# Gate and query products of a hybrid decoder step by seven block products for each pair, with gates and retention's output kept in DRAM

## The chip, the cores and the metric

The kernel runs on one core of one Trainium2 chip. The metric is the device time of one execution in microseconds (us), as the median of several runs. All arithmetic is on 32-bit floats. Matrix products are made on TensorE from operands that are split into a rounded part and a remainder (fp32r), so that one product of full precision takes three matmuls: rounded x rounded, rounded x remainder, remainder x rounded.

## The reference, cut to what matters

Two layers work on 512 prompt tokens and 64 sample tokens (8 sequences of 8), 1024 channels:

```
rq, rk, rv, rg, sq, sk, sv, mq, g_ret, g_swa, g_mem = split(x @ w_in)
ret_b = (silu(rg) * group_norm(retention(rq, rk, rv))) @ w_br_ret
swa_b = window_attention(sq, sk, sv) @ w_br_swa
mem_b = memory_attention(mq, mem_k, mem_v) @ w_br_mem
merged = sigmoid(g_ret) * ret_b + sigmoid(g_swa) * swa_b + sigmoid(g_mem) * mem_b
x = layer_norm(ALPHA * x + merged @ w_out)
h = square(relu(x @ w_up))
x = layer_norm(ALPHA * x + h @ w_down)
```

The three gates are 1024 channels wide each, mq is 512 wide.

## The kernel before, in words

Activations lie channel by token, in two groups of 288 tokens, A and B (32 sample and 256 prompt tokens each). Weights come as units of 128 x 8 x 128 numbers, 154 for a layer, in the order of `unit_order`: a unit multiplies 1024 input channels into 128 output channels, or (`bs`, `bm`, `dh`) 512 into 256. `fetch` loads a raw unit on SP's queue; `split` turns it into the rounded half (ScalarE or VectorE) and the remainder, either by one VectorE subtraction or, for units split more than FAR us ahead, by a negated copy on ScalarE and an accumulating DMA of the raw weights issued by GpSimd. `mstep` multiplies a unit with one token group (24 matmuls of 288 columns, or 12 for half the input channels) into a PSUM bank of tag `g`, of which there are three, and hands it to an evacuation function; `both` does so for A and B.

The instructions of each engine stand in the order in which the program is written. `run` writes a list of steps. After each six matmuls `Filler.advance` is called, which inserts pieces of other work: generators for retention, window attention (`swa_prompt`, `swa_sample`), memory attention (`mem_prompt`, `mem_sample`) and norms, each cut at its yields and continued when a built-in estimate of the engines' times says that its operands are nearly ready. Generators of one lane go one after the other. `finish` and `drain` write what is left of them at once. `tick` splits weights ahead, up to `2 * cap` halves alive.

All larger tiles share one pool of 38 buffers (tag `T`). PSUM banks of tag `a` (five) serve attention and retention.

In `layer` the order is: memory keys and values (mk, mv), retention's inputs with retention beside them, sv, sk, sq; then a `drain`; then eight times a unit of gr and a unit of br (window attention beside it); four units of mq; four times two units of gs and one of bs (memory attention beside it); four times two of gm and one of bm; wo with the first norm; up; down. A gate is Tanh of its product, kept in one of four small tiles `t` until the branch's product is evacuated: `br_ev` writes (t + 1) * product into `mg`, `add_ev` adds to it and, for bm, writes the rounded half and the remainder that wo reads.

The up product of the later six eighths is made by `pair_steps`: two units are multiplied with both groups by seven block products of 12 matmuls, in place of eight (Winograd's form of Strassen's scheme, blocks: two output units by two halves of the input channels; token groups A and B). `block` makes the seven weight operands of a pair from its two raw units, three of them sums; `sums` makes the four sums of activation blocks. In `pair_steps` the seven products are combined by subtractions on VectorE. There, each pair is followed by two units of dh.

Of the kernel before, what the change touches and what calls it, by code (L numbers as in the profile page):

```python
# [32 lines left out]
ORDER_DH = (0, 2, 1, 3)  # L33
SKEW_WO = 8
# [5 lines left out]
FAR = 11.0  # L40
DN_SKEW = 7
# [25 lines left out]
def unit_order():  # L67
# [21 lines left out]
def pack_weights(w_in, w_br_ret, w_br_swa, w_br_mem, w_out, w_mem_kv, w_up, w_down):  # L89
# [13 lines left out]
    for l in range(DEPTH):  # L103
        wb_swa = w_br_swa[l][swa_rows]
        for u, key in enumerate(order):
# [29 lines left out]
            elif k == "up":  # L135
                v = full(w_up[l], m * P + np.arange(P))
            elif k in ("ua", "ub"):
# [88 lines left out]
def items():  # L226


    r = []
    for l in range(DEPTH):  # L230
        for i, k in enumerate(unit_order()):
            u = l * UNITS + i
            if k[0] == "ua":
                r += [(u + 1, (l,) + k, b) for b in range(BLOCKS)]
            elif k[0] != "ub":
                r.append((u, (l,) + k, None))
    return r


def plan(todo):  # L240
# [3 lines left out]
    while i < len(todo):  # L244
# [12 lines left out]
        else:  # L257
            out.append(t)
            t += {"mk": c, "mv": c, "ua": n / 2}.get(k, 2 * n)
# [190 lines left out]
class Builder:  # L450
# [24 lines left out]
    def dram(self, shape):  # L475
        self.n += 1
        return self.dr.tile(shape, F32, tag=f"d{self.n}", name=f"d{self.n}", bufs=1)
# [73 lines left out]
    def split(self, i):  # L551
# [8 lines left out]
        if self.use[i] - self.fill.t > FAR and k[1] not in ("mq", "gs", "bs", "gm", "bm") and u > 15 \  # L560
# [9 lines left out]
    def block(self, u, b):  # L570


        V = self.nc.vector
        ra, rb = self.raw[u - 1], self.raw[u]
# [14 lines left out]
        if b == 5 and self.items[self.split_next][1][2] == 7:  # L589
# [70 lines left out]

    def pair_steps(self, key, XT, evac):

# [42 lines left out]
        def e6():  # L705
# [3 lines left out]
                step(2, lambda: (bank("x", "a"), True, e2)), step(3, lambda: (bank("y", "a"), True, e3)),  # L709
# [3 lines left out]
    def sums(self, y, T):  # L713
# [4 lines left out]
        for h in range(2):  # L718
            q = slice(2 * h, 2 * h + 2)
            b11, b21, b12, b22 = y["A"][0][:, q], y["A"][1][:, q], y["B"][0][:, q], y["B"][1][:, q]  # L720
# [7 lines left out]
            for i in range(2):  # L728
# [3 lines left out]
                V.tensor_tensor(t[i][1], r[i], t[i][0].bitcast(F32), ALU.subtract)  # L732

# [283 lines left out]
    def retention(self, l, p, qk, rv, rvs, sg, GR):  # L1017
# [159 lines left out]
        for g_ in "AB":  # L1177
# [4 lines left out]
            self.nc.vector.tensor_tensor(lo, src, hi.bitcast(F32), ALU.subtract)  # L1182

# [35 lines left out]
    def swa_prompt(self, l, c, sq, sk, sv, SW):  # L1219
# [62 lines left out]
        for kb in range(kb0, 2):  # L1282
            for kv in range(2):
# [3 lines left out]
        yield from self.hi_lo(SW[g]["h"][0][:, :, a:a + P], SW[g]["l"][0][:, :, a:a + P],  # L1287
                              ps.rearrange("p (i q) -> p i q", i=4))

    def swa_sample(self, l, sq, sk, svs, SW):  # L1290
# [43 lines left out]
        for f in range(2):  # L1334
# [13 lines left out]
            cs = slice(SOFF[g], SOFF[g] + 32)  # L1348
            hi = SW[g]["h"][0][:, :, cs].rearrange("p g (b t) -> p g b t", b=4)
            lo = SW[g]["l"][0][:, :, cs].rearrange("p g (b t) -> p g b t", b=4)  # L1350
            yield from self.hi_lo(hi, lo, o)
# [129 lines left out]
    def layer(self, l, X):  # L1481
# [3 lines left out]
        uid = {k: self.item[(l,) + k, None] for k in unit_order() if k[0] not in ("ua", "ub")}  # L1485
# [64 lines left out]

        GR = {g: {"h": [], "l": []} for g in "AB"}
# [123 lines left out]
        steps += self.both(uid["sv", 0], X, sv_ev) + self.both(uid["sk", 0], X, sk_ev)  # L1675
        for m in range(4):
# [6 lines left out]
        mg = [self.pair_tiles(), self.pair_tiles()]  # L1683
        SW = self.feat_tiles(1)
        for c in range(4):
            self.fill.add(self.swa_prompt(l, c, sq, sk, sv, SW), 3)
        self.fill.add(self.swa_sample(l, sq, sk, svs, SW), 3)
        ts = {}

        def gate_ev(m):  # L1690
            def ev(g, ps):
                t = self.tt()[:, :NG[g]]
# [278 lines left out]
```

## Time and profile before

| | |
|---|---|
| median of 3 runs | 2159.79 us (2156.87 to 2160.55) |
| the profiled execution | 2157.69 us |
| its span, first to last instruction | 2155.9 us |
| granted TensorE clock, mean share | 0.992 |
| TensorE busy | 2118.5 us, 98% |
| VectorE, ScalarE, GpSimd busy | 59%, 43%, 11% |
| DMA | 292.42 MB, mean 136 GB/s |

The span leaves out what lies around the first and the last instruction. Busy times of pipelined instructions overlap by some hundredths of a us each.

### The profile page before, as it was taken

The numbers are of one execution on the slowest core, as the hardware profiler recorded it, in microseconds if no ns is written. First come the engines' busy times: TensorE is split into PE (matmuls) and PEld (weight loads), VectorE is DVE, ScalarE is ACT, GpSimd is POOL, SyncE is SP. The second block draws the span as 40 slices with busy tenths as digits, with TensorE's granted clock in tenths as the row PEclk, the third lists the DMA queues.
The fourth block names the chain that finished last, engine by engine and source line by source line (L and its number), as shares of the span: only waits on it lengthen the run. The fifth ranks groups of instructions, "written<-read, shape, count | busy, mean of one in ns | idle before, by whom it ended". The sixth has DMA issues, their size and how long they took to land.

```text
span 2155.9 us, 39206 instructions
## 1 busy us (share of the span) xinstructions
PE 2118.5 (98%) x16180; PEld 2058.2 (95%) x16180; DVE 1261.5 (59%) x2705; ACT 925.6 (43%) x1750; POOL 232.9 (11%) x297
## 2 busy tenths in 40 slices
PE   9999999999999999999989999999999999999997
PEld 8999999999999999999989999999999999999997
DVE  6455644456547576765745556444565565767766
ACT  4333355322256444446553333562221665444452
POOL 0111111000022000000321111000000220000012
PEclk9999999999999999999999999999999999999999
DMA  8455645434375422225895556544342854222242
GB/s 316 114 143 134 166 118 120 145 109 144 119 211 127 126 94 84 79 88 151 204 266 143 144 141 174 122 114 132 135 157 85 229 120 130 79 79 99 98 122 60
DMA packets 87618, 292.42 MB, mean 136 GB/s; under 512 B 9552, under 2 KB 19280, under 8 KB 87376
## 3 DMA queue, kind: packets, MB, share of 16 engines
q0 software_dynamic: 31408, 113.79, 24.0%
q1 hardware_dynamic: 50944, 168.27, 22.8%
q10 hardware_dynamic: 5088, 7.87, 1.1%
q8 instruction: 127, 2.08, 0.4%
q14 instruction: 51, 0.42, 0.1%
HBM read 200.89 MB, written 15.99 MB: 101 GB/s over the span
## 4 chain that ended last, share of the span: by engine, by line
PE 91%; DVE 4%; issue 2%; DMA 2%; ACT 1%; POOL 0%; SPq 0%; DVEq 0%; POOLq 0%; ACTq 0%
PE pg L359 69%; PE pa L359 23%; DVE T L359 3%; DMA T<-T 1%; ACT T L359 1%; DVE u L359 0%; DMA T<-in_wall 0%; ACT u L359 0%; DMA T<-in_memT 0%; SPq L359 0%; DVE ln L359 0%; DVE accA L359 0%; DVE s L359 0%; POOL T L359 0%; POOL rc L359 0%
## 5 line engine op out<-in xcount | busy, mean ns | idle before, releaser
L359 PE MATMUL pg<-T,T 128*128 128x288 f32 (+1 forms) x11840 | 1643.3, 297 | 19.3 <-ACT T L359 10.9
L359 PEld LDWEIGHTS pg<-T,T 128*128 128x128 f32 x11840 | 1591.4, 190 | 44.4 <-ACT T L359 17.0
L359 PE MATMUL pa<-T,T 128*128 128x288 f32 (+8 forms) x3368 | 449.5, 303 | 2.4 <-DVE u L359 2.4
L359 ACT CAST T<-T 128x1024 fp32r<-128x1024 f32 (+6 forms) x464 | 354.6, 789 | 210.1 <-DVE T L359 174.7
L359 PEld LDWEIGHTS pa<-T,T 128*128 128x128 f32 (+3 forms) x3368 | 399.7, 176 | 23.0 <-issue 9.5
L359 DVE TENSOR_TENSOR T<-T,T 128x512 fp32r<-128x512 f32 (+8 forms) x418 | 361.9, 878 | 85.2 <-ACT T L359 75.4
L359 POOL DMA_DIRECT2D T<-T x145 | 124.7, 868 | 1379.2 <-ACT T L359 1013.2
L359 ACT ACTIVATE T<-T 128x1024 fp32r<-128x1024 f32 (+2 forms) x157 | 165.3, 1054 | 10.5 <-DVE T L359 8.2
L359 ACT ACTIVATE t<-pg 128x288 f32<-128x288 f32 x128 | 52.6, 411 | 215.8 <-PE pg L359 210.5
L359 ACT ACTIVATE u<-u 128x288 f32<-128x288 f32 x200 | 89.0, 445 | 96.0 <-DVE u L359 92.0
L359 DVE TENSOR_TENSOR T<-u,T 128x288 fp32r<-128x288 f32 x160 | 72.4, 454 | 78.0 <-ACT T L359 78.0
L359 ACT COPY T<-pg 128x512 f32<-128x512 f32 (+2 forms) x44 | 20.8, 479 | 213.0 <-PE pg L359 213.0
L359 DVE TENSOR_TENSOR T<-T,pg 128x288 f32<-128x288 f32 x128 | 57.7, 451 | 75.6 <-PE pg L359 75.1
L359 ACT CAST T<-u 128x288 fp32r<-128x288 f32 x160 | 69.3, 433 | 52.6 <-DVE u L359 48.6
L359 DVE TENSOR_TENSOR T<-T,u 128x288 f32<-128x288 f32 (+2 forms) x136 | 88.1, 660 | 3.8
L359 DVE SCALAR_TENSOR_TENSOR T<-t,pg 128x288 f32<-128x288 f32 x64 | 29.0, 453 | 94.0 <-ACT t L359 76.2
L359 DVE TENSOR_TENSOR T<-T,pa 128x288 f32<-128x288 f32 (+1 forms) x92 | 52.1, 567 | 25.1 <-PE pa L359 23.7
L359 DVE TENSOR_TENSOR T<-pa,T 128x512 fp32r<-128x512 f32 (+2 forms) x48 | 24.9, 533 | 64.9 <-ACT T L359 64.7
L359 DVE SCALAR_TENSOR_TENSOR u<-t,pg 128x288 f32<-128x288 f32 x64 | 28.8, 450 | 55.8 <-PE pg L359 55.2
L359 DVE TENSOR_TENSOR u<-u,pa 128x288 f32<-128x288 f32 x72 | 32.6, 453 | 35.2 <-PE pa L359 35.0
L359 ACT CAST T<-pa 128x512 fp32r<-128x512 f32 (+2 forms) x44 | 19.4, 451 | 70.2 <-PE pa L359 66.3
L359 DVE CAST T<-T 128x1024 fp32r<-128x1024 f32 (+1 forms) x71 | 45.2, 641 | 1.0 <-DMA T<-in_wall 1.0
(164 smaller groups left out, 1095.3 us busy)
## 6 DMA issues: line engine op xcount, KB each, us to landing
T<-in_wall SPq DMA_DIRECT2D x305, 512.0 KB, 4.2
T<-T POOLq DMA_DIRECT2D x141, 512.0 KB, 5.7
T<-in_mck POOLq DMA_DIRECT2D x16, 512.0 KB, 4.4
T<-in_mcv POOLq DMA_DIRECT2D x16, 512.0 KB, 6.6
T<-in_s POOLq DMA_DIRECT2D x8, 512.0 KB, 8.2
out_state_s<-T POOLq DMA_DIRECT2D x8, 512.0 KB, 3.8
T<-in_xT SPq DMA_DIRECT2D x4, 576.0 KB, 10.4
T<-in_xT ACTq DMA_DIRECT2D x4, 576.0 KB, 6.8
```

Source lines behind the costliest of these rows:

```text
L359: r = f(*a, **kw)
```

## The change

The 24 gate units and the four of mq become 14 pairs (`xa`, `xb` in the weights' order), multiplied by `pair_steps` in one stage behind sq: four pairs of gs, four of gr, four of gm, two of mq. Weight blocks 0, 4 and 5 of a pair get their remainder from ScalarE and an accumulating DMA where they are split more than 8 us ahead. The sums of x's blocks are made by `sums` from x in DRAM, loaded anew on GpSimd's queue, from the third unit of sq on. The Tanh of a pair's products goes into one tile and from there to DRAM by ScalarE's queue; it is loaded again on SP's queue a step before its use. Retention's output `GR` is stored to DRAM by GpSimd's queue and loaded before the last bs unit has run; window attention's output goes through DRAM too. Behind the pairs come bs (four units), br (eight) and bm (four) without gates between them, memory attention beside bs and br. mk and mv are reloaded by GpSimd's queue in place of ScalarE's. The diff, cut:

```diff
+PAIRS = [((k, 2 * i), (k, 2 * i + 1)) for k, n in (("gs", 4), ("gr", 4), ("gm", 4), ("mq", 2)) for i in range(n)]
+FAR_BLOCK = 8.0
@@ unit_order
-    for m in range(8):
-        o += [("gr", m), ("br", m)]
-    o += [("mq", m) for m in range(4)]
-    for g, b in (("gs", "bs"), ("gm", "bm")):
-        for i in range(4):
-            o += [(g, 2 * i), (g, 2 * i + 1), (b, i)]
+    for j in range(len(PAIRS)):
+        o += [("xa", j), ("xb", j)]
+    o += [("bs", i) for i in range(4)] + [("br", m) for m in range(8)] + [("bm", i) for i in range(4)]
@@ split
-        if self.use[i] - self.fill.t > FAR and k[1] not in ("mq", "gs", "bs", "gm", "bm") and u > 15 \
+        if self.use[i] - self.fill.t > FAR and k[1] not in ("bs", "br") and u > 15 \
                 and (k[1] != "dh" or k[2] == 0):
@@ block
+        key, far = self.items[self.split_next][1], self.use[self.split_next] - self.fill.t
...
-        if b == 5 and self.items[self.split_next][1][2] == 7:
+        if b == 5 and key[1:3] == ("ua", 7) or b in (0, 4, 5) and key[1] == "xa" and far > FAR_BLOCK:
             self.nc.scalar.activation(w[:, 4:8], src, AF.Copy, scale=-1.0)
             self.nc.gpsimd.dma_start(w[:, 4:8], src, accum_op=ALU.add)
@@ pair_steps
-    def pair_steps(self, key, XT, evac):
+    def pair_steps(self, key, XT, evac, xbank="a"):
...
-                step(2, lambda: (bank("x", "a"), True, e2)), step(3, lambda: (bank("y", "a"), True, e3)),
+                step(2, lambda: (bank("x", xbank), True, e2)), step(3, lambda: (bank("y", "a"), True, e3)),
@@ sums
-    def sums(self, y, T):
+    def sums(self, parts, T):
...
+            b11, b21, b12, b22 = parts(h)
+            yield (b11, b21, b12, b22)
@@ retention, at the end
+            if p % 2:
+                for k in "hl":
+                    nc.gpsimd.dma_start(self.grd[g_, k, p // 2], GR[g_][k][p // 2])
@@ swa_prompt, at the end (swa_sample alike)
-        yield from self.hi_lo(SW[g]["h"][0][:, :, a:a + P], SW[g]["l"][0][:, :, a:a + P],
-                              ps.rearrange("p (i q) -> p i q", i=4))
+        st = self.tile([P, 2, 4, P], F32R)
+        yield from self.hi_lo(st[:, 0], st[:, 1], ps.rearrange("p (i q) -> p i q", i=4))
+        nc.gpsimd.dma_start(SW[:, :, :, OFF[g] + a:OFF[g] + a + P], st)
@@ layer
+        def reload(h):
+            t = [self.tile([P, 4, 288]) for _ in range(2)]
+            for i, g in enumerate("AB"):
+                for j in range(2):
+                    nc.gpsimd.dma_start(t[i][:, 2 * j:2 * j + 2],
+                                        src[:, 4 * j + 2 * h:4 * j + 2 * h + 2, OFF[g]:OFF[g] + NG[g]])
+            return [t[i][:, 2 * j:2 * j + 2] for i in range(2) for j in range(2)]
+        tx = self.sums(reload, Ts)
         for m in range(4):
...
+            if m == 2:
+                steps.append(([], lambda: self.fill.add(tx, 1), 0.0))
             steps += self.both(uid["sq", m], X, sq_ev)
+        del GR
         self.run(steps)
         self.fill.drain()
...
+        def gate_pair(j):
+            st = []
+            def ev(i, g, ps):
+                if not st:
+                    st.append(self.tile([P, 4, 288]))
+                S.activation(st[0][:, 2 * i + "AB".index(g)], ps, AF.Tanh, scale=0.5)
+                if (i, g) == (0, "B"):
+                    nc.scalar.dma_start(gd[j], st.pop())
             return ev
...
+        for j in range(12):
+            steps += self.pair_steps((l, "xa", j), XT, gate_pair(j), "g")
+        steps.append(([], load_sw, 0.0))
+        for j in range(2):
+            steps += self.pair_steps((l, "xa", 12 + j), XT, mq_pair(j), "g")
+            if j == 0:
+                steps.append(([], lambda: self.fill.add(mem_parts(), 2), 0.0))
+        self.run(steps, 3.5)
         self.fill.drain()
+        del X, XT, Ts, sq, sk, sv, svs, skv
...
+        def gate(j):
+            def fn():
+                t = self.tile([P, 4, 288])
+                nc.sync.dma_start(t, gd[j])
...
+        def load_gr():
+            for h in range(2):
+                for g in "AB":
+                    for k in "hl":
+                        t = self.tile([P, 4, 288], F32R)
+                        nc.gpsimd.dma_start(t, self.grd[g, k, h])
+                        GR[g][k].append(t)
+        steps = [gate(0)]
         for i in range(4):
-            for m in (2 * i, 2 * i + 1):
-                steps += self.both(uid["gs", m], X, gate_ev(m))
+            steps.append(gate(i + 1))
             for e in range(2):
-                steps += self.both(uid["bs", i], SW, add_ev(2 * i + e), range(4 * e, 4 * e + 4))
+                steps += self.both(uid["bs", i], SW, first_ev(2 * i + e), range(4 * e, 4 * e + 4))
+            if i == 2:
+                steps.append(([], load_gr, 0.0))
         self.run(steps, 2.5)
...
+        for m in range(8):
+            if m % 2 == 0:
+                steps.append(gate(5 + m // 2))
+            steps += self.both(uid["br", m], GR, add_ev(1, m))
+        steps.append(([], lambda: [self.fill.finish(gen) for gen in mem], 0.0))
+        self.run(steps, 2.5)
...
         for i in range(4):
+            if i < 3:
+                steps.append(gate(9 + i))
             if i == 3:
                 steps.append(([], load_y, 0.0))
-            for m in (2 * i, 2 * i + 1):
-                steps += self.both(uid["gm", m], X, gate_ev(m))
-            if i == 0:
-                steps.append(([], lambda: [self.fill.finish(gen) for gen in mem], 0.0))
             for e in range(2):
-                steps += self.both(uid["bm", i], ME, add_ev(2 * i + e, M2), range(4 * e, 4 * e + 4))
+                steps += self.both(uid["bm", i], ME, add_ev(2, 2 * i + e, M2), range(4 * e, 4 * e + 4))
```

`first_ev` writes (t + 1) * product into `mg`, as `br_ev` did; `load_sw` drains the fillers and loads window attention's output by four GpSimd transfers.

## Rows read from the trace of the kernel before

**Rows 1.** The page: busy time of the engines, granted clock in 40 slices.

```profile
PE 2118.5 (98%) x16180; PEld 2058.2 (95%) x16180; DVE 1261.5 (59%) x2705; ACT 925.6 (43%) x1750; POOL 232.9 (11%) x297
...
PEclk9999999999999999999999999999999999999999
```

**Rows 2.** Timeline, ScalarE among gm units: start, length (us), engine, operation, idle before.

```profile
566.51 0.41 ACT L359 ACTIVATE t<-pg 128x288 f32<-128x288 f32 x1 [2.79 <-PE pg L359]
569.71 0.41 ACT L359 ACTIVATE t<-pg 128x288 f32<-128x288 f32 x1 [2.79 <-PE pg L359]
```

**Rows 3.** Windows: gr/br; gs/bs with memory attention; start and rest of pairs.

```profile
core 0: us, PE busy (x) PEld busy (x) DVE busy (x) ACT busy (x) POOL busy (x), PEclk, DMA share, GB/s
...
727.00:750.00 23.00, 23.00 (x175) 23.00 (x174) 20.70 (x34) 8.19 (x11) 1.11 (x3) 1.00 0.43 112
750.00:996.00 246.00, 246.00 (x1847) 246.00 (x1847) 173.00 (x308) 105.70 (x214) 0.90 (x1) 1.00 0.28 92
283.30:407.50 124.20, 124.20 (x976) 118.27 (x974) 56.15 (x132) 68.08 (x151) 12.12 (x15) 1.00 0.52 128
437.00:551.00 114.00, 113.52 (x979) 109.50 (x978) 67.84 (x151) 31.04 (x83) 8.82 (x16) 1.00 0.43 148
```

**Rows 4.** Instruction groups by shape: count, busy us, mean ns, idle before.

```profile
L359 DVE TENSOR_TENSOR T<-T,T 128x512 fp32r<-128x512 f32 x144 | 98.0, 687 | 32.3 <-ACT T L359 31.8
L359 ACT CAST T<-T 128x512 fp32r<-128x512 f32 x148 | 87.3, 618 | 128.8 <-DVE T L359 120.0 <-PE pg L359 4.4 <-DMA T<-in_memT 4.4
L359 ACT ACTIVATE t<-pg 128x288 f32<-128x288 f32 x128 | 52.6, 411 | 215.8 <-PE pg L359 210.5 <-issue 4.9
L359 DVE TENSOR_TENSOR T<-T,T 128x1024 f32<-128x1024 f32 x24 | 29.2, 1218 | 0.0
L359 DVE TENSOR_TENSOR u<-pg,u 128x288 f32<-128x288 f32 x24 | 11.0, 457 | 3.2 <-PE pg L359 3.2
```

**Rows 5.** Timeline, first layer: first and last instructions of the sums behind up.

```profile
727.64 2.88 DVE L359 TENSOR_TENSOR T<-T,T 128x576 f32<-128x576 f32 x4
...
740.68 1.95 DVE L359 TENSOR_TENSOR T<-T,T 128x1152 fp32r<-128x1152 f32 x2
```

**Rows 6.** DMA: software queue's packets, MB, share; issues with KB, landing; GpSimd's issue time.

```profile
q0 software_dynamic: 31408, 113.79, 24.0%
...
T<-in_wall SPq DMA_DIRECT2D x305, 512.0 KB, 4.2
T<-T POOLq DMA_DIRECT2D x141, 512.0 KB, 5.7
...
L359 POOL DMA_DIRECT2D T<-T x145 | 124.7, 868 | 1379.2 <-ACT T L359 1013.2 <-PE pg L359 268.0 <-PE pa L359 54.7
```

**Rows 7.** Timeline, end of sq: retention's last remainders, the last rope.

```profile
273.54 1.42 DVE L359 TENSOR_TENSOR T<-T,T 128x576 fp32r<-128x576 f32 x2
...
281.54 0.48 DVE L359 STREAM_SHUFFLE u<-pg 128x288 f32<-128x288 f32 x1
```

**Rows 8.** Timeline, memory attention: first step, start of second sample part, last step.

```profile
437.16 0.71 ACT L359 CAST T<-T 128x256 fp32r<-128x256 f32 x2
...
538.33 0.89 DVE L359 TENSOR_TENSOR T<-T,cst 128x128 f32<-128x128 f32 x4
...
550.75 0.29 DVE L359 TENSOR_TENSOR T<-pa,T 128x128 fp32r<-128x128 f32 x1 [0.72 <-ACT T L359]
```

**Rows 9.** Timeline, bm: two evacuations in a row; ScalarE's reloads of x.

```profile
571.32 0.45 DVE L359 SCALAR_TENSOR_TENSOR u<-t,pg 128x288 f32<-128x288 f32 x1 [5.71 <-PE pg L359]
573.14 0.45 DVE L359 SCALAR_TENSOR_TENSOR u<-t,pg 128x288 f32<-128x288 f32 x1
...
596.95 2.62 ACTq L359 DMA_DIRECT2D T<-in_xT  x4
```

**Rows 10.** Windows of 10 us with TensorE idle: columns as in Rows 3.

```profile
1010.00:1020.00 10.00, 7.06 (x49) 6.39 (x48) 4.77 (x10) 7.13 (x14) 0.84 (x1) 1.00 0.96 297
1080.00:1090.00 10.00, 7.11 (x38) 6.15 (x37) 2.81 (x5) 6.41 (x10) 3.79 (x5) 0.83 1.02 276
```

More of the change, by code (lines that the diff above doesn't have):

```diff
@@ L136, in pack_weights @@
                 v = full(w_up[l], m * P + np.arange(P))
+            elif k in ("xa", "xb"):
+                f, g = (full(w_in[l], COLS[c] + i * P + np.arange(P)) for c, i in PAIRS[m])
+                if k == "xb":
+                    f, g = g, f
+                v = np.concatenate([f[:, :4], g[:, 4:]], 1)
             elif k in ("ua", "ub"):
@@ L732, in sums, with operands, part, tsum @@
                 V.tensor_tensor(t[i][1], r[i], t[i][0].bitcast(F32), ALU.subtract)
+    @staticmethod
+    def operands(X, T):
+        def part(g, j):
+            return lambda i: (X[g]["h"][j][:, i, :], X[g]["l"][j][:, i, :])
+        def tsum(a, b):
+            return lambda i: tuple(T[i // 2][a][e][:, 2 * b + i % 2, :] for e in range(2))
+        return [part("A", 0), tsum(1, 0), tsum(0, 1), tsum(0, 0), part("A", 1), tsum(1, 1), part("B", 1)]
     def pair_tiles(self, dt=F32):
@@ L1347, in swa_sample @@
             g = "AB"[f]
[L1348 to L1351, printed above, removed]
+            st = self.u(256).bitcast(F32R).rearrange("p (k g t) -> p k g t", k=2, g=4)
+            yield from self.hi_lo(*(st[:, k].rearrange("p g (b t) -> p g b t", b=4) for k in range(2)), o)
+            nc.gpsimd.dma_start(SW[:, :, :, f * 544:f * 544 + 32], st)
     def mem_prompt(self, h, mq, mk, mv, ME, ahead=None):
@@ L1484, in layer @@
         ident = self.c("ident")
-        uid = {k: self.item[(l,) + k, None] for k in unit_order() if k[0] not in ("ua", "ub")}
+        uid = {k: self.item[(l,) + k, None] for k in unit_order() if k[0] not in ("ua", "ub", "xa", "xb")}
         M = self.M
@@ L1549, in layer @@
         self.run(steps, 2 * CAP_M if l else CAP_M)
+        self.grd = {(g, k, h): self.dram([P, 4, 288], F32R) for g in "AB" for k in "hl" for h in range(2)}
+        swd = self.dram([P, 2, 4, TOK], F32R)
+        gd = [self.dram([P, 4, 288]) for _ in range(12)]
+        src = self.I["xT"] if l == 0 else self.xs
         GR = {g: {"h": [], "l": []} for g in "AB"}
@@ L1715, in mem_parts, with load_sw @@
                 yield (parts[0],)
[L1716 to L1724 removed]
+                V.tensor_tensor(parts[1], t, parts[0].bitcast(F32), ALU.subtract)
+        SW = {g: {} for g in "AB"}
+        def load_sw():
+            self.fill.drain()
+            for g in "AB":
+                for i, k in enumerate("hl"):
+                    SW[g][k] = [self.tile([P, 4, 288], F32R)]
+                    nc.gpsimd.dma_start(SW[g][k][0], swd[:, i, :, OFF[g]:OFF[g] + NG[g]])
+        steps = []
+        for j in range(12):
[6 more added lines that the diff above has]
+        self.run(steps, 3.5)
         self.fill.drain()
+        del X, XT, Ts, sq, sk, sv, svs, skv
         ME = self.feat_tiles(1)
@@ L1823, in layer @@
         Ts = []
-        tg = self.sums(y, Ts)
+        tg = self.sums(lambda h: [y[g][j][:, 2 * h:2 * h + 2] for g in "AB" for j in range(2)], Ts)
         def dh(q, k, src):
@@ L1848, in layer @@
         del tg
-        def part(g, j):
-            return lambda i: (X1[g]["h"][j][:, i, :], X1[g]["l"][j][:, i, :])
-        def tsum(a, b):
-            return lambda i: tuple(Ts[i // 2][a][e][:, 2 * b + i % 2, :] for e in range(2))
-        XT = [part("A", 0), tsum(1, 0), tsum(0, 1), tsum(0, 0), part("A", 1), tsum(1, 1), part("B", 1)]
-        for k in "hl":
-            X1["B"][k][0] = None
+        XT = self.operands(X1, Ts)
         H.pop(0)
```

77 lines of the change are left out of this document (35 added, 42 removed).

## The prediction

> **What bounds the kernel now.** First the totals on the page [rows 1]: TensorE is busy for 2118.5 of 2155.9 us, at a granted clock that stands at nine tenths or more in every slice; the other engines have room. So a matmul fewer is worth its own time, if nothing new makes TensorE wait. Next the pace: in the gm stage one gate product (24 matmuls of 288 columns) ends every 3.20 us [rows 2], 0.133 us a matmul; I use 1.60 us for 12 matmuls and 6.40 us for a unit (48). Third, the stretches of the first layer that are rearranged [rows 3]: TensorE is busy for 124.20 of 124.20 us where gates and br alternate and for 113.52 of 114.00 where memory attention runs. Nothing waits there now, so there is nothing to gain but matmuls, and every wait that the new order makes is a loss.
>
> **What is removed.** 24 gate units and 4 of mq become 14 pairs in each layer. A pair of units took 2 x 48 = 96 matmuls and takes 7 x 12 = 84 afterwards, all of 288 columns. That is 12 x 14 x 2 = 336 matmuls fewer, 28 x 1.60 = 44.8 us: 22.4 a layer. From the profiled execution's 2157.69 us this alone gives 2112.9.
>
> **What is added, per layer.**
>
> *VectorE and ScalarE in the pair stage.* A pair needs seven remainders of 512 elements (0.687 each), one sum of 1024 (1.218), two of 512 and five subtractions of 288 (0.457) [rows 4]: 4.81 + 1.22 + 1.37 + 2.29 = 9.7 us of VectorE. Window attention runs beside it; in the first stretch of [rows 3] VectorE was busy for 56.15 us, of which 16 evacuations of about 0.45 are br's, so at most 49 us are attention, 4.1 a pair over 12 pairs. TensorE has 11.2 us a pair, and attention's matmuls (124.2 - 16 x 6.4 = 21.8 us) add 1.8: 13.0. VectorE asks for 13.8, or 11.7 where the three remainders of blocks 0, 4 and 5 go to ScalarE and GpSimd (3 x 0.687 less). The nearest row is the start of the existing pair stage, where VectorE was busy for 20.70 of 23.00 us, 90%, and TensorE all 23.00 [rows 3]. 11.7 of 13.0 is the same 90%. ScalarE has seven casts (0.618), a copy, four Tanh (0.411), the three extra passes and attention, some 8 + 2.5 us, and fits. So from 0 to 12 x 0.8 = 9 us; I take **1**, since the row at 90% lost nothing.
>
> *Start of the pair stage.* Block 1 needs the sums of x from both halves, 1.6 us after the stage begins; block 0 alone covers them. The same sums stand in the trace behind up: from 727.64 to 742.63, some 15 us beside other work [rows 5], within a stage of four units (25.6 us). Now they are started two units ahead (12.8 us), and first their data must be reloaded: four issues on GpSimd's queue a half, 0.87 us each, and a landing of 4 to 6 us (5.7 for the nearest transfers) [rows 6]. VectorE meanwhile ropes sq until 283 and retention's last remainders end at 275 [rows 7]; retention's output is now stored by four more issues of the same GpSimd queue, ahead of the second half's reload. By these rows the first half's data land near 277, its chain ends near 284, the second half's near 288 to 291, where block 1 wants them at 283.6. Below: 0, if the second half is loaded while the first is summed; above: 9. I take **5**. Queued behind the waiting matmuls is the whole pair stage, but nothing else is late: weights catch up meanwhile.
>
> *Order bs, br, bm instead of gates between.* Memory attention took from 437.16 to 550.75 us [rows 8], 113.6 us, beside 14 units and its own matmuls (114 - 89.6 = 24 us), and was just finished when bm wanted it. Now 12 units lie before bm: 76.8 + 24 = 101 us. At the old pace 12.8 us are left, the whole second sample part, which began at 538.33 [rows 8]. It is then forced in order on TensorE, which waits for VectorE, ScalarE and four loads between its own 4 to 5 us: some 8 us idle. On the other side, retention's output is reloaded behind the third bs unit by eight GpSimd issues of 0.87 us, 4.7 MB. The software queue moved 113.79 MB in 24.0% of the span [rows 6], 220 GB/s, so the six tiles that br's first group needs take 16 us after the first issue, and one bs unit with attention covers 8: up to 8 us, or nothing if GpSimd runs ahead of TensorE and the buffers are free. The two are not added in full, since a wait for the reload gives attention time: 0 to 14 together, I take **5**. Gates come back by 12 loads on SP, each a unit or more ahead (landing 4.2 us [rows 6]); the first has three PSUM banks of 1.6 us as cover, so 0. VectorE's evacuations are as many as before.
>
> *End of bm.* Sixteen evacuations of 1.60 us of matmuls follow one another, where four did with 12.8 us of gates between. VectorE needs 1.82 us from one to the next [rows 9], since the remainder waits for ScalarE's cast: 16 x 0.22 = 3.5 us late at the end, of which the last group B (1.6 us) hides a part before wo asks for group A. The four reloads of x held ScalarE for 2.62 us before [rows 9], in a gap; now in the last bm unit. 0 to 6, I take **2**.
>
> *Clock.* What a wait costs beyond itself: in 1080 to 1090 us TensorE idled 2.9 us and the granted mean was 0.83 (half speed for part of it), 1.7 us lost; in 1010 to 1020 us it idled as long and kept 1.00 [rows 10]. Four such places a layer, 0 to 7, I take **1**, because the waits forecast are mostly pieces of 1 to 3 us. The Trainium skill (TensorE: Matmul & The Clock Gate, Part 1) puts it harder: throttled is the default and activity lifts it, so every wait would cost a half-speed stretch. Only the first of the two rows agrees; by the rule the sum would be 6 us a layer worse, 2153, inside the handed-back case below, which gets 0.03 of its chance from it.
>
> *Costed at nothing:* the stores of gates (0.66 us of ScalarE each by the four issues of [rows 9], in the room above), attention's output through memory (needed 22 us later, behind two mq pairs), and some 61 MB of transfers, a fifth more than now: the engines of the queues are half busy in these stretches [rows 3].
>
> **Sum.** 22.4 - (1 + 5 + 5 + 2 + 1) = 8.4 a layer, 16.8 in all: 2157.7 - 16.8 = 2141. The profiled execution lies 2.1 us below the median of 2159.79; from there it is 2143. I predict 2142 us, 0.8% faster.
>
> **Rivals.**
> *The gain is kept.* Waits are hidden: sums loaded early, GpSimd ahead, attention faster beside br. For it: TensorE idles only 0.5 us in all the rearranged stretches now [rows 3], with VectorE at 45 to 60%. Against it: the two-unit lead before a 15 us chain. Waits of 2 to 5 us a layer give 2117 to 2122; the case takes in 2113 to 2130.
> *The gain is handed back.* The matmuls go, idle takes their place: 14 us at br and bm, 8 at the sums. For it: the 12.8 us of attention that have no cover; against it: partial cover of each. 2157.7 - 44.8 + 2 x 22 = 2157; the case takes in 2152 to 2166.
> *Slower: buffers.* One pool of 38 buffers serves all. In the pair stage x holds 8, its sums 8, sq 2, sk/sv 1, mq 2; the other 17 are for raw weights (4), their sums, up to 7 split blocks, a gate or two and attention's 4 to 6. If a raw weight must wait for a buffer, its landing (4.2 us) comes late and every pair waits. It decides from 22.4 / 14 = 1.6 us a pair, or 0.7 with the other terms; at 1 us a pair 2169, at 2 us 2197. For it: this count; against it: the existing pair stage holds about as many (26, and 12 for weights) and TensorE ran 246.00 of 246.00 us [rows 3].
>
> **Chances and range.** Forecast (2130 to 2152) 0.42, gain kept 0.25, handed back 0.18, slower by buffers 0.15. 0.2%, 4.3 us, is about what a measurement of this kernel tells from no change: 2155.5 to 2164.1. Of the handed-back case 0.03 lies below it, 0.11 within and 0.04 above. Faster 0.70, same 0.11, slower 0.19. From 2119 to 2172 about a tenth is left out at each end; the forecast's own range is 2130 to 2152.
>
> **What would show it.** TensorE's matmuls fall by 336 and its busy time by some 45 us. Its idle time in the layers tells the terms: a gap of about 5 us within 3 us after sq's last matmul, ended by VectorE; none over 1 us between pairs; gaps before br's first group (ended by a GpSimd load) and before bm (VectorE, ScalarE); about 2 us at wo's start. SP's weight loads shall land as early as before; if blocks wait for them in every pair, the buffers are it. If the gaps after sq and before bm are missing, the gain is kept. The prediction is wrong if idle grows by under 10 or over 45 us.

## Result and profile after

The changed kernel takes 2314.3 us (2313.3 to 2315.1, 4 runs) beside 2159.5 us (2156.9 to 2160.6, 4 runs) of the kernel before: a ratio of 1.0719 (95% interval 1.0700 to 1.0737). It is slower by 155 us where some 18 us less were forecast.

The page of the profiled execution (span 2312.2 us), its lines on busy time and the 40 slices, beside [rows 1]:

```profile
PE 2128.8 (92%) x15844; PEld 2046.9 (89%) x15844; DVE 1422.9 (62%) x3003; ACT 1040.3 (45%) x2017; POOL 326.3 (14%) x424
...
PE   9999979849989999999989997997599899999997
...
PEclk9999989969989999999999998998699899999999
```

The 336 matmuls are gone (16180 to 15844), and yet TensorE is busy for 10.3 us more. Without them it should be 2118.5 - 44.8 = 2073.7, so the matmuls that are left take 55 us longer. Most of that is the lower of TensorE's two clock levels (1.2 and 2.4 GHz): added up from the clock records of the two traces, TensorE was busy at that level for 118 us, and for 22 us before. Half of it is lost, 59 us beside 11, which makes 48 of the 55; the other 7 stay open. Its idle time (span less busy) rose from 37.4 to 183.4 us. So 146 us of new idle time and 55 of longer matmuls, less 44.8, make the 156 us between the two spans. Slices 6, 8, 9 and 25, 28, 29 of TensorE, each some 58 us long, show where: the start and the end of the pairs in each layer.

The windows of the first layer (columns as in [rows 3]): the start of the pairs, a stretch within the 12 gate pairs, and the stretch around their end.

```profile
283.60:299.50 15.90, 1.45 (x10) 1.09 (x9) 8.37 (x14) 3.00 (x4) 4.31 (x6) 0.64 0.63 194
303.00:433.00 130.00, 124.81 (x894) 120.02 (x894) 86.43 (x164) 86.84 (x198) 26.20 (x31) 0.98 0.76 192
440.00:520.00 80.00, 40.79 (x292) 33.63 (x293) 39.16 (x89) 31.38 (x85) 8.09 (x11) 0.70 0.33 77
```

In 440 to 520 TensorE is busy for half the time, and the mean granted clock is 0.70. What it waited for, from the view of waits for 283 to 700 us (engine, tile, releaser: us in total, times, longest):

```profile
PE pa L363 <- DVE T L363: 34.7, 9, 13.5
PE pg L363 <- ACT T L363: 16.0, 2, 14.5
PE pa L363 <- DMA T<-in_swk: 8.7, 1, 8.7
PE pg L363 <- DVE u L363: 6.6, 8, 3.7
```

The first and third lines are mostly window attention, which was not finished when the reload before mq drained it. The timeline of TensorE there (start, length, operation, idle time before it):

```profile
468.95 3.73 PE L363 MATMUL pa<-cst,T 128*128 128x128 f32 x16 [13.48 <-DVE T L363]
...
477.67 2.57 PE L363 MATMUL pa<-T,T 128*128 128x256 f32 x16 [3.12 <-DVE T L363]
488.87 3.93 PE L363 MATMUL pa<-cst,T 128*128 128x128 f32 x16 [8.63 <-DVE T L363]
...
503.40 2.09 PE L363 MATMUL pa<-T,u 64*32 64x128 f32 x64 [8.70 <-DMA T<-in_swk]
510.15 1.94 PE L363 MATMUL pa<-cst,T 128*128 128x128 f32 x8 [4.66 <-DVE T L363]
```

The pieces are one and a half prompt chunks and the sample part: 39.0 us of idle time in all, and 38.7 in the second layer. The second line of the waits is the start of the pairs. TensorE, VectorE and GpSimd there:

```profile
265.96 3.24 POOL L363 DMA_DIRECT2D T<-in_xT  x4
...
284.03 0.53 POOL L363 DMA_DIRECT2D d<-T  x1 [3.99 <-DVE T L363]
284.62 0.87 POOL L363 DMA_DIRECT2D T<-T  x1
285.19 3.22 POOL L363 DMA_DIRECT2D T<-in_xT  x4
```
```profile
295.32 0.76 DVE L363 TENSOR_TENSOR T<-T 128x576 f32<-128x576 f32 x1 [7.45 <-DMA T<-in_xT]
```
```profile
299.50 5.92 PE L363 MATMUL pg<-T,T 128*128 128x288 f32 x22 [14.46 <-ACT T L363]
```

The second half of x is asked for at 285.19 us, behind retention's last store; VectorE has it at 295.32, and TensorE waits 14.46 us (15.01 in the second layer). Where the idle time lies, added up from such lines:

| place | layer 1 | layer 2 |
|---|---|---|
| start of the pairs (sums of x) | 14.5 | 15.0 |
| within the 12 gate pairs | 5.8 | 7.3 |
| window attention forced before mq | 39.0 | 38.7 |
| mq's pairs | 1.4 | 4.2 |
| memory attention forced before bm | 6.5 | 6.5 |
| bm to wo | 2.8 | 3.7 |

SP's weights land as before, counted from their issue: T<-in_wall takes 4.5 us, where [rows 6] has 4.2.

### The profile page after: what moved, and what is told of

It is laid out like the page before. It is cut to its first block, busy times and chain, and to the rows that moved or that the text cites. A ratio compares the mean times of both kernels' runs of the same rounds, so it can differ in the third digit from the quotient of the medians.

```text
span 2312.2 us, 39583 instructions
## 1 busy us (share of the span) xinstructions
PE 2128.8 (92%) x15844; PEld 2046.9 (89%) x15844; DVE 1422.9 (62%) x3003; ACT 1040.3 (45%) x2017; POOL 326.3 (14%) x424
## 4 chain that ended last, share of the span: by engine, by line
PE 69%; issue 10%; DVE 9%; ACT 6%; DMA 4%; POOL 1%; ACTq 0%; SPq 0%; DVEq 0%; POOLq 0%
PE pg L363 47%; PE pa L363 22%; DVE T L363 5%; ACT T L363 5%; DVE u L363 2%; DMA T<-T 1%; DMA T<-d 1%; POOL T L363 1%; DMA T<-in_wall 1%; ACT u L363 1%; DVE m L363 1%; DMA T<-in_swk 1%; DMA T<-in_xT 0%; DVE s L363 0%; POOL d L363 0%
## 5 line engine op out<-in xcount | busy, mean ns | idle before, releaser
L363 PE MATMUL pg<-T,T 128*128 128x288 f32 (+1 forms) x10832 | 1536.5, 300 | 68.6 <-ACT T L363 44.2
L363 PEld LDWEIGHTS pg<-T,T 128*128 128x128 f32 x10832 | 1474.6, 192 | 98.8 <-ACT T L363 54.9
L363 PE MATMUL pa<-T,T 128*128 128x288 f32 (+9 forms) x4040 | 563.6, 312 | 24.6 <-DVE T L363 15.0
L363 ACT CAST T<-T 128x512 fp32r<-128x512 f32 (+7 forms) x619 | 440.8, 732 | 256.4 <-DVE T L363 209.6
L363 PEld LDWEIGHTS pa<-T,T 128*128 128x128 f32 (+3 forms) x4040 | 502.0, 183 | 54.8 <-DVE T L363 13.5
L363 DVE TENSOR_TENSOR T<-T,T 128x512 fp32r<-128x512 f32 (+8 forms) x522 | 438.3, 851 | 126.4 <-ACT T L363 122.2
L363 POOL DMA_DIRECT2D T<-T x201 | 172.7, 869 | 1350.2 <-ACT T L363 841.4
L363 PE MATMUL pa<-cst,T 128*128 128x128 f32 (+1 forms) x306 | 49.2, 313 | 53.6 <-DVE T L363 53.6
L363 PEld LDWEIGHTS pa<-cst,T 128*128 128x128 f32 (+1 forms) x306 | 41.0, 156 | 57.1 <-issue 54.7
L363 DVE SCALAR_TENSOR_TENSOR T<-t,pg 128x288 f32<-128x288 f32 x32 | 14.5, 454 | 75.9 <-ACT t L363 75.9
L363 ACT ACTIVATE T<-u 128x288 f32<-128x288 f32 x72 | 31.7, 441 | 59.7 <-DVE u L363 59.5
```

Of the source, the lines that this page charges most:

```text
L363: r = f(*a, **kw)
```

## Experiments

Theory 1: window attention is slowed beside the pairs and its rest is forced (1a, after the first runs: because VectorE's queue stands still behind ScalarE). Theory 2: VectorE and ScalarE lack room for the pair stage in any case. Theory 3: the sums of x start too late. The rival to all three: the new order and the DRAM trips. Times are single runs beside a run of the kernel before (2155 to 2160 us) unless an interval stands with them. The twelve runs of one and the same kernel spread over 13 and 15 us in two cases below (2144.9 to 2157.9, 2151.0 to 2166.1), so a smaller difference between two single runs shows nothing by itself.

**Without window attention**, in the changed kernel and in the one before:

```diff
-        for c in range(4):
-            self.fill.add(self.swa_prompt(l, c, sq, sk, sv, swd), 3)
-        self.fill.add(self.swa_sample(l, sq, sk, svs, swd), 3)
+        for g in "AB":
+            for i, k in enumerate("hl"):
+                nc.gpsimd.dma_start(swd[:, i, :, OFF[g]:OFF[g] + NG[g]], X[g][k][0])
```

> The changed kernel without window attention (its output is filled from x instead, so the result is not the reference's). Theory 1 (window attention's chain of dependent steps is slowed beside the pairs, its rest is forced before mq): the idle 39 us of TensorE before mq and the half speed around it go in each layer, with attention's own matmuls (about 22 us a layer): 2314 - 2 x (39 + 22) - about 40 of half speed = 2150, and pairs come every 11.2 to 12 us. Theory 2 (the pair stage is short of VectorE and ScalarE with or without attention): pairs come every 13.5 us or more, 14 x 2.3 = 32 us a layer are still lost, 2190 or above. Theory 3 (the sums of x come late): the gap of some 15 us at the start of the pairs stays in both.

> The kernel before without window attention (its output filled from x, not the reference's). The base for the run above: TensorE was never idle beside attention there, so attention costs its matmuls alone, some 22 us a layer: 2158 - 44 = 2114. If theory 1 holds, the changed kernel without attention stands at this + at most 35 us (sums' gaps of 30, the rest at br, bm and wo some 20, less 45 for the matmuls, plus half speed); by theory 2 at this + 75 or more.

Measured: 2154.5 and 2104.5 us. Attention costs 54 us in the kernel before and 160 in the changed one: 106 of the 155 us. But without it the changed kernel is still 50 us behind, not 45 ahead. That lies between the 35 of theory 1 and the 75 of theory 2; part of it the next run finds in the order. From 303 to 433 us 937 matmuls ran, 84 a pair: a pair took 11.65 us, so theory 2's 13.5 is out. The gap at the start stayed (14.22 us).

**The order alone**, with direct products for gates and mq:

```diff
-            steps += self.pair_steps((l, "xa", j), XT, gate_pair(j), "g")
+            steps += plain(j, gate_pair(j))
```

> The new order and all its trips through DRAM, but gates and mq as direct products as in the kernel before (no pairs, no sums of x). Theories 1 and 2 both put the loss down to the pairs: window attention finishes beside 24 direct units (154 us of matmuls), no wait above 2 us before mq; what stays is the order's own (br, bm, wo: some 10 us a layer): 2165 to 2185. If the order or the DRAM trips are the cause (rival): 2220 or above, with waits before br and bm or ended by DMA.

Measured: 2199.6 us, 41 above the kernel before. Window attention finished in time; the order itself costs more than forecast. TensorE's timeline at the end of memory attention and at wo:

```profile
586.81 1.21 PE L363 MATMUL pa<-T,T 128*128 128x512 f32 x4 [1.66 <-DVE T L363]
590.00 3.60 PE L363 MATMUL pa<-T,T 128*32 128x256 f32 x32 [1.98 <-DVE T L363]
595.00 0.44 PE L363 MATMUL pa<-cst,u 128*128 128x128 f32 x2 [1.40 <-ACT u L363]
...
628.36 1.16 PE L363 MATMUL pg<-T,T 128*128 128x288 f32 x7 [1.19 <-DVE u L363]
631.04 1.33 PE L363 MATMUL pg<-T,T 128*128 128x288 f32 x4 [1.52 <-ACT T L363]
```

The pairs then cost 115 us on top of it (2314 - 2200).

**Window attention in two lanes**: chunks 0 and 2 beside chunks 1 and 3.

```diff
-            self.fill.add(self.swa_prompt(l, c, sq, sk, sv, swd), 3)
+            self.fill.add(self.swa_prompt(l, c, sq, sk, sv, swd), 3 + c % 2)
```

> The changed kernel with window attention's four prompt chunks in two lanes (two chunks advance side by side instead of one after the other). Theory 1: the work is the same, only the dependent chain is no longer alone, so more of it is done beside the 12 pairs and the forced rest before mq shrinks from 39 us a layer to under 15: 2314 - 2 x 25 - some half speed = 2240 to 2270. Theory 2: VectorE and ScalarE are full, so the attention that is done earlier makes the pairs later by as much: 2295 to 2320.

Measured: 2285.4 us, 29 less, between the two. Forced waits of over 1 us before mq fall to 1.70 and 4.69, but the pairs now wait for VectorE. Waits from 303 to 433 us:

```profile
PE pg L363 <- DVE u L363: 13.5, 5, 3.1
PE pa L363 <- DVE u L363: 2.2, 2, 1.5
```

In the changed kernel that was 5.1 us. So attention does take something from the pairs. What VectorE itself waits for there, in the changed kernel:

```profile
DVE T L363 <- ACT T L363: 34.4, 30, 2.4
DVE u L363 <- PE pa L363: 3.9, 6, 1.5
DVE u L363 <- PE pg L363: 3.3, 2, 1.9
```

VectorE is busy for 86.4 of the 130 us, 66%, and stands still for another 34.4 behind ScalarE: together 93%. Only 7.2 us are waits for TensorE. In the kernel before, beside the same attention (283 to 408 us), the sum was 56.8 + 41.6 of 125 us, 79%, and 23 us were waits for TensorE:

```profile
DVE m L359 <- ACT T L359: 25.9, 5, 6.8
DVE T L359 <- ACT T L359: 15.7, 4, 4.7
DVE T L359 <- PE pa L359: 14.2, 9, 3.9
DVE T L359 <- PE pg L359: 8.9, 11, 2.0
```

The Trainium skill (Perfetto Trace Analysis, Identifying the Most-Contended Engine) takes occupancy as a fair measure of how close VectorE is to its roofline. The 66% may be that, but it does not tell how much more work fits into this queue; busy time and waits for ScalarE together come closer. How one such wait reaches TensorE, on VectorE's and then TensorE's timeline:

```profile
384.44 0.69 DVE L363 TENSOR_TENSOR T<-s,T 128x512 fp32r<-128x512 f32 x1 [0.68 <-ACT T L363]
385.05 1.21 DVE L363 TENSOR_REDUCE m<-T 128x4 f32<-128x1024 f32 x1
386.18 0.45 DVE L363 TENSOR_TENSOR u<-u,pg 128x288 f32<-128x288 f32 x1
```
```profile
386.68 2.97 PE L363 MATMUL pg<-T,T 128*128 128x288 f32 x12 [3.67 <-DVE u L363]
```

A remainder stands behind ScalarE's cast of the same block, attention's maximum behind the remainder, and the subtraction that frees a PSUM bank last.

**The remainder one block later:**

```diff
         self.nc.scalar.copy(w[:, 0:4], src)
+        self.rest()
...
+        elif key[1] == "xa":
+            hold = ra, rb, b and (sa, sb)
+            self.pend = self.split_next, lambda: (hold, V.tensor_tensor(w[:, 4:8], src, w[:, 0:4].bitcast(F32), ALU.subtract))
```

`rest` writes what is pending; `run` calls it where a step uses that block.

> The changed kernel with one edit: in the 14 pairs of a layer VectorE's remainder of a weight block is written behind the cast of the block after it, not right behind its own. The same instructions, only VectorE no longer stands at once behind ScalarE. Between 303 and 433 us of the changed kernel VectorE is busy for 86 of 130 us and waits another 34.4 us, 30 times, for ScalarE's casts. Theory 1a (the waits in VectorE's queue take the room that window attention needed): they fall below 12 us, attention gets the rest (some 25 us of VectorE a layer of the 49 it wants), and the forced 39 us before mq shrink to 15 to 20: 2314 - 2 x 22 - about 20 of half speed = 2240 to 2265. Theory 2 (VectorE's work itself is too much): the waits move to other rows and the time stays within 10 us, 2304 to 2320.

Measured: 2287.2 us, 27 less, between the two theories. From 303 to 433 us:

```profile
303.00:433.00 130.00, 127.89 (x940) 124.26 (x940) 94.08 (x175) 91.35 (x206) 27.90 (x33) 0.99 0.82 200
```
```profile
DVE T L363 <- ACT T L363: 21.2, 24, 3.3
```

VectorE does 7.7 us more and waits 13 us less, so the waits did take room. But the gain went to the pairs (the gate pairs end 6.6 us sooner); the forced waits before mq only fall from 39 to 34 us (33 in the second layer). So VectorE's waits alone do not explain why attention is left over: its single lane of dependent steps is still too slow. How much of it is written beside the pairs is decided as the program is written, by the built-in estimate; no run changed that estimate alone.

**Earlier sums:** `if m == 2` becomes `if m == 0` where `tx` is added.

> The changed kernel with the sums of x started before sq's first unit, two units (12.8 us) earlier. Theory 3 (the sums start too late): the gap of 14.5 us at the start of the pairs shrinks to 2 or less, in each layer, with 4 us of half speed: 2314 - 2 x 16 = 2275 to 2285. Rival (the gap only moves: VectorE and ScalarE, which make the first weight blocks at the same time, are what the first pairs wait for): less than half of it is gained, 2295 to 2315.

Measured: 2290.7 us, 24 less. The gap of 14.46 us became two of 1.62 and 3.45, ended by ScalarE and VectorE, which then made the first weight blocks. The time lies between theory 3 and its rival: the gap goes for the most part, with a rest as the rival said.

**All of it**, with memory attention in two lanes too (`3 + i // 4`), and memory's lanes alone in the order with direct products:

> Late remainders, early sums, window attention in two lanes and memory attention in two lanes together. If the causes found are the whole loss and independent: 2314 less 45 to 70 (late remainders) less 30 (sums) less 29 (two lanes, as measured) less 10 to 15 (memory attention): 2170 to 2200, above the kernel before still. If VectorE is simply full in the pair stage, each repair gives its time back to another wait: 2240 or above.

> The new order with direct products (2199.6 as one run gave it) and memory attention's two halves side by side in two lanes. Its last sample part was forced behind br there: 6 to 7 us idle of TensorE a layer between 584 and 601 us, and 0.89 of the granted clock in 570 to 600. If the order's loss of 41 us is mainly that tail: 2199.6 - 2 x 10 = 2175 to 2185. If the loss lies elsewhere (loads of gates, bm's end): above 2192.

Measured: 2196.9 and 2182.6 us. The first is 117 less than the changed kernel, 20 more than the parts one by one (27 + 24 + 29, and 17 for memory's lanes). A likely reason is that two lanes need the room that late remainders make: from 303 to 433 us TensorE waits 6.2 us for the subtractions here, and 15.7 with two lanes alone. No run has just these two edits, so this is argued and not shown. VectorE now works 100 of 130 us:

```profile
303.00:433.00 130.00, 123.59 (x898) 117.91 (x897) 100.33 (x197) 93.54 (x231) 26.14 (x31) 0.99 0.74 186
```

**Fewer pairs.** Where attention keeps VectorE busy, the gates are direct; only the last eight pairs (half of gr, gm, mq) are block products. First a base: group A of the last bm units ahead of group B.

```diff
+PLAIN = 6
-        o += [("xa", j), ("xb", j)]
+        o += [("xa", j), ("xb", j)] if j >= PLAIN else list(PAIRS[j])
...
+            if j == 2:
+                steps.append(([], lambda: self.fill.add(tx, 1), 0.0))
...
+            steps += self.pair_steps((l, "xa", j), XT, gate_pair(j), "g") if j >= PLAIN else plain(j, gate_pair(j))
```

> The run with direct products and memory attention in two lanes (2182.6), with one edit more: the last two bm units make all products of group A before those of group B, so that wo's group A has group B's matmuls as cover. The waits at wo's start were 0.76 + 1.52 us in the first layer and 1.88 + 1.52 in the second, with half speed behind them: if the order's loss lies there, 2182.6 - 2 x 4 = 2174 to 2178. Rival (the waits only move to a later weight): 2181 or above. It is the base for the next run.

> The new order with all repairs (late remainders, attention in two lanes, group A of bm first), the first 12 gate units (gs, and half of gr) as direct products, and only the last eight pairs by block products; the sums of x start beside the direct units; the two pairs of mq keep all remainders on VectorE; up to eight weight halves are split ahead in the stage. If window attention needs VectorE's room and nothing else (theory 1a), it gets most of its work done beside the direct units, where VectorE was busy for 40 of 130 us, and the eight pairs keep their 1.6 us each: about 2176 - 2 x 12.8 = 2145 to 2160. If pairs cost their gain wherever they stand: 2170 or above, no better than with direct products.

Measured: 2181.1 us, as the rival said: TensorE now waited 1.75 us in bm for a remainder that a copy and an accumulating DMA make (3.36 in the second layer), and 1.34 at wo. And with eight pairs 2163.6 us, a ratio of 1.0029 (1.0011 to 1.0046) to the kernel before, so still a little slower. Against the single run with direct products that is 17.5 us less, of 25.6 for the matmuls. VectorE in bm, in this run:

```profile
589.65 0.45 DVE L364 SCALAR_TENSOR_TENSOR u<-T,pg 128x288 f32<-128x288 f32 x1
...
591.09 0.46 DVE L364 TENSOR_TENSOR T<-u,T 128x288 fp32r<-128x288 f32 x1 [0.50 <-ACT T L364]
591.47 0.45 DVE L364 SCALAR_TENSOR_TENSOR u<-T,pg 128x288 f32<-128x288 f32 x1
```

The same wait again: 1.82 us from one evacuation to the next, as [rows 9] had it, against 1.60 of matmuls. So the cure went there too, with the other edits that its expectation names; also, only the last bm unit now has group A ahead:

```diff
-                    self.fill.later(lambda: V.tensor_tensor(lo, w, h.bitcast(F32), ALU.subtract), 1.5, h)
+                    self.rest()
+                    self.pend = 10 ** 9, lambda: V.tensor_tensor(lo, w, h.bitcast(F32), ALU.subtract)
```

> The kernel with six direct pairs and eight block pairs (2163.6), and the same cure at two more places: in bm VectorE's remainder of an evacuation is written behind the next evacuation's operations (VectorE took 1.84 us from one to the next there, of them 0.5 waiting for ScalarE's cast, against 1.60 us of matmuls), and the first three wo units get their remainder from VectorE, not from a copy and a DMA (waits of 1.39 + 0.73 + 1.36 us in the first layer, 3.36 + 0.61 in the second). The sample part of window attention lets its two loads land before its products are written (waits of 1.77 and 2.53). Theory 1a (a remainder right behind its cast costs VectorE's queue the cast's time, and the order's loss sits at those waits): 2163.6 - 5.3 - 6.5 - about 5 of half speed = 2144 to 2151, faster than the kernel before. Rival (the order costs that by its DMA traffic, whatever waits): 2158 to 2165.

> The same edits, but all 14 pairs by block products (window attention beside 12 pairs, as in the change). If waits in queues alone were the loss, six pairs more give 6 x 1.6 x 2 = 19 us on the run above: 2125 to 2132. If the pair stage has no room for all of window attention, as theory 2 has it (VectorE was busy for 100 of 130 us in the run with all repairs, and the stage still lost some 15 us a layer), it is slower than the run above by 20 to 40 us: 2165 to 2190.

Measured: 2152.5 us, 0.9987 (0.9970 to 1.0005), between theory and rival and not to be told from the kernel before. No wait over 0.2 us is left in bm and at wo in the first layer; 0.47 and 1.04 us are left in the second. With all 14 pairs it is 2164.4 us in one run: six pairs more cost 12 us, and more than any of the twelve runs took, where they should give 19. Whether the pairs or attention beside them lose that:

> The kernel with all 14 pairs and every cure (2164.4), without window attention (its output filled from x, not the reference's). In the kernel before attention costs 54 us (2158.7 - 2104.5). Theory 2 in its narrower form (VectorE has no room for pairs and all of window attention at once, the pairs alone fit): the missing 31 us (12 more where 19 less were due) go with attention, 2164 - 54 - 31 = 2075 to 2085. Rival (the pairs themselves lose it): 2164 - 54 = 2105 to 2115.

> The changed kernel without window attention and without the transfers that stood for it (the bs units read retention's stored output instead: not the reference's result). With the transfers it took 2154.5. If they caused the waits for DMA in the pairs and before mq (some 8 us in the first layer): 2138 to 2146. If those waits are the pairs' own: 2150 to 2156. The 14 us wait for the sums of x stays in both.

> All 14 pairs, every cure, no window attention and no transfers for it (bs reads retention's stored output). With the transfers 2103.6, with a wait of 6.64 and 6.70 us in the two layers behind them and half speed after it. If the pairs alone fit (theory 2, narrower form): 2103.6 - 2 x (6.7 + 3) = 2080 to 2087, that is 18 to 24 below the kernel before without attention (2104.5), which makes window attention beside all 14 pairs cost 78 to 84 instead of 54. If the pairs themselves lose their gain: 2095 to 2104.

Measured: 2103.6, 2152.1 and 2083.5 us. The transfers that stood for attention had spoilt the first (a wait of 6.64 us), but not the runs of the changed kernel (2154.5 and 2152.1). Without them, waits and window from 303 to 433 us of the kernel with every cure:

```profile
303.00:433.00 130.00, 130.00 (x1002) 130.00 (x1001) 88.23 (x148) 85.20 (x172) 28.14 (x35) 1.00 0.84 231
```
```profile
DVE u L363 <- PE pg L363: 29.1, 33, 2.1
...
DVE T L363 <- ACT T L363: 0.8, 2, 0.4
```

Now VectorE waits for TensorE, and TensorE never idles in this stretch: the pairs alone fit. The changed kernel without attention has 31.5 us in the place of the 0.8. The difference is not the late remainders' alone, since this kernel has the other cures too. And in the changed kernel those 31.5 us cost little without attention: TensorE was busy for 125.68 of the 130 us, and its waits there were ended by transfers, not by VectorE:

```profile
303.00:433.00 130.00, 125.68 (x925) 124.31 (x925) 79.22 (x134) 80.28 (x167) 28.18 (x34) 0.99 0.77 199
```

It is attention and the pairs together that lose. Attention on top costs 81 us (2164.4 - 2083.5) where it cost 54 before; that is 27 of the 31 us. With it, VectorE in the kernel with every cure:

```profile
303.00:433.00 130.00, 127.36 (x982) 120.66 (x981) 103.56 (x208) 96.15 (x236) 29.21 (x35) 0.99 0.77 195
```
```profile
DVE T L363 <- ACT T L363: 15.6, 17, 2.3
```

Busy time and waits are 119 of 130 us again, and in the second layer a wait of 4.61 us is still forced before mq, with a granted clock of 0.73 from 1520 to 1545 us. This agrees with theory 2 in its narrower form. Of the 27 us, 11 are idle time by the pages, and some 15 the lower clock level by the clock records; that VectorE's room is behind all of it is argued, not shown.

**A version that beats both.** The eight-pair kernel, with two sample parts that let their loads land (`yield 7.0` and `yield 2.0` ahead of their products), and the same with nine pairs:

> The eight-pair kernel (0.9987 of before) with two small edits: window attention's sample part lets its loads land for 7 us, not 3, before its products are written (TensorE waited 2.41 and 2.51 us for them), and memory attention's sample part lets its values land for 2 us (1.91 us). Theory: about 4 us a layer with half speed, 0.995 to 0.998 of before, faster. Rival (waits move): 0.998 to 1.0.

> The same with five direct pairs and nine block pairs, 24 matmuls or 3.2 us a layer... 12 matmuls, 1.6 us a layer less. If VectorE has room for a ninth pair beside window attention: 3 us less than the eight-pair run, 0.993 to 0.997. If attention is then forced or the pairs wait for VectorE: 0.998 or above.

Measured: 2145.0 us with eight, 0.9951 (0.9935 to 0.9967) of the kernel before, and 2149.6 with nine, 0.9968 (0.9956 to 0.9980). Both are faster, by 0.5% and 0.3%, clear of noise (5 and 12 runs); a ninth pair brings nothing that shows. Of the eight-pair kernel, windows as above:

```profile
283.60:299.50 15.90, 15.90 (x124) 15.90 (x123) 10.72 (x28) 11.88 (x30) 1.70 (x2) 1.00 0.68 147
303.00:433.00 130.00, 129.62 (x1024) 122.53 (x1023) 80.73 (x156) 85.25 (x187) 30.80 (x38) 1.00 0.86 208
440.00:520.00 80.00, 79.12 (x595) 78.13 (x594) 59.39 (x121) 36.03 (x87) 12.37 (x21) 1.00 0.82 265
```

## Why the prediction was wrong

*What is removed* was right: 336 matmuls, 44.8 us.

*VectorE and ScalarE in the pair stage: 1, range 0 to 9.* This is the step that failed. It compared VectorE's busy time (11.7 us a pair) with TensorE's time (13.0) and took the start of the up pairs as proof that 90% loses nothing; but there the other 10%, 2.3 us, was all that waits could be. It counted no wait of VectorE for ScalarE, and that is 34.4 us in 130, about 3 us a pair. The first rows to doubt it by were there: [rows 4] puts 31.8 us of waits for ScalarE before the same remainders. The second half of the step fell as well: *attention's output through memory* was costed at nothing, since attention would be done by then as in [rows 3]. It was not, and 39 us a layer were forced. The runs without it show that attention costs 106 to 108 us more than before, of the 155. Why it was not done has two parts that the runs show, and neither is enough alone. With late remainders 27 us went, but 34 us a layer were still forced. With attention in two lanes 29 us went and about 7 us were forced, but TensorE's waits for the subtractions between the pairs rose from 5.1 to 15.7 us in 130. How the 106 us split between the two stays open.

*Start of the pair stage: 5, range 0 to 9.* The mechanism was right (sums late behind retention's stores on GpSimd's queue), its size was not: 14.5 and 15.0 us idle, outside the range. The forecast let the second half's data land at 288 to 291 us; VectorE had them at 295.32, since the issues ended only at 288.4. Two units more of lead took 24 us off.

*br, bm and the end of bm: 5 + 2 a layer.* Right in kind: memory attention's sample part was forced, 6.5 us, and bm's evacuations lag, 2.8 to 3.7 us. With direct products, where nothing else is changed, the order costs 41 us in all, 20 a layer with half speed; two lanes for memory attention took back 17 of it, and of the other 24 some 15 are idle time by the page (52.9 us beside 37.4). The reload of retention's output, the other half of the term, made no wait over 1 us in the changed kernel.

*Clock: 1, range 0 to 7.* Some 24 us a layer by the clock records, 27 if all of the longer matmuls are counted. The row taken (1010 to 1020 us at full clock) was read as one of pieces of 1 to 3 us, but its waits are 1.19, 0.87 and 0.88 us. In the changed kernel 640 to 656 us, with three waits of 1.40 to 1.99 us, were granted 0.70, and so was the stretch of the forced waits of 3 to 13 us; the start of the pairs, with one wait of 14.46 us, was granted 0.64. The Trainium skill (TensorE: Matmul & The Clock Gate, Part 1) says that the array is throttled unless activity lifts it; here the trace agrees, with 48 us in all, 24 a layer, where the prediction's estimate by that rule was 6 a layer. That every wait costs a half-speed stretch was the prediction's own reading of the rule, and it does not hold here: around single waits of 0.80 and 1.39 us (the first two windows) the granted clock stayed at 1.00.

```profile
318.00:328.00 10.00, 9.20 (x69) 8.96 (x68) 5.45 (x11) 7.42 (x22) 2.52 (x3) 1.00 0.78 183
540.00:548.00 8.00, 6.61 (x50) 6.37 (x49) 5.66 (x8) 1.89 (x4) 0.00 (x0) 1.00 1.02 414
640.00:656.00 16.00, 9.97 (x103) 5.72 (x105) 7.51 (x22) 2.29 (x6) 0.00 (x0) 0.70 0.74 276
```

*The rivals.* No engine waited for a raw weight: from 303 to 433 us none of the waits of TensorE, VectorE and ScalarE is ended by T<-in_wall. With every cure and without attention, which needs some of the buffers, the pairs ran 130.00 of 130 us in the same pool. So the forecast's own way to a slower kernel does not show, and the true one, VectorE's queue, stood among the terms, with a range of 9 us that took VectorE's lag as the only loss and not what attention leaves undone. The bound above should have been all of attention's remaining work in order on an idle TensorE.

*What stays open:* the all-cures kernel without attention gains 21 us over 2104.5, not 45. Of the 24 us that are missing, 20 are idle time by the pages (58.6 us beside 38.9). Gaps at the start of its pairs (2.06 and 3.51 us, at a granted clock of 0.69) and the order's rest are part of that. A larger pool of buffers wasn't tried, nor late remainders and two lanes of window attention without the other cures.

## What to carry to other kernels

Before work is put on an engine with a fixed order, add its waits for its partner to its busy time, from the view of waits of the nearest stretch: VectorE at 66% had 93% of its time taken, and attention beside the pairs was not done in time. Where one engine rounds and another subtracts, write the subtraction one step later than the rounding: alone, that took VectorE's waits for ScalarE from 34.4 us in 130 to 21.2, and with the other cures and without attention they went from 31.5 to 0.8. And if other work has to finish beside a stage, ask what happens when it doesn't: here it was drained on an idle TensorE, and keeping the plain products where that work runs and the cheaper ones behind it, with the other cures, made the kernel 0.5% faster than before.

## What was not expected of the hardware

Half speed cost about a third of the idle time that came with it: 48 us beside 146. And loads on GpSimd's queue landed later than a lead of 3 us covers: in the eight-pair kernel TensorE waited 2.41 and 2.51 us for window attention's keys, and 0.38 and 0.84 with 7 us.
